# GpSimd's rotary steps at their traced pace, a fourth seven-product chunk in two stages, and q, k ahead of V in the second mixer

## The chip, the core and the metric

The kernel runs on one core of one Trainium2 chip, in one launch. The metric is the device time of that launch in microseconds. A core has TensorE (PE, with its weight loads as PEld), VectorE (DVE), ScalarE (ACT), GpSimd (POOL) and SyncE (SP), each with an in-order queue of its own, and 16 DMA engines that all queues share.

## The reference

A two-layer streaming encoder on 256 tokens of width 1024, in f32, with a memory of 256 entries. Cut to what matters:

```python
for i in range(2):
    x = x + 0.5 * swiglu(rmsnorm(x), gate, up, down)             # 1024 -> 2816 -> 1024
    q, k, v, q_m = split(rmsnorm(x) @ w_in[i], [768, 1536, 2304])
    k_m, v_m = split(rmsnorm(mem) @ w_mem_kv[i], 2)
    o_m = memory_attention(norm(q_m), norm(k_m), v_m)             # 4 heads of 64
    if i == 0:
        o_s = chunked_attention(norm(q), norm(k), v, rel_bias)    # 12 heads
    else:                                                         # 6 heads of two halves
        q, k = rotary(norm(q), positions), rotary(norm(k), positions)
        o_s = norm(softmax(q1 k1) v - lam * softmax(q2 k2) v)
    x = x + concat(o_s, o_m) @ w_out[i]
    x = x + 0.5 * swiglu(rmsnorm(x), gate2, up2, down2)
```

The rotary angles are position times inverse frequency, reduced by 2 pi, then sine and cosine.

## The kernel before

**Products.** Every large product is done in f32 by three passes: both sides are split into a high half `hi` (rounded to fp32r by ScalarE, line 417) and a low half `lo` (the rest, by VectorE, line 438), and TensorE adds hi x hi, hi x lo and lo x hi into one PSUM bank (`dense`, lines 596, 599, 602, each 128 x 128 by 512 columns). Weights come by DMA in chunks of 1 MB into 3 raw buffers; split chunks stand in 4 pairs of hi and lo buffers.

**Stages.** For each layer: FFN 1 (gate and up products, then `down` over 11 chunks), the mixer, FFN 2. A stage is named (layer, 1 or 2). In the first layer the keys and values of the memory for both layers (`memory_kv`) stand between FFN 1 and the mixer; their left sides are `memh` and `meml`. A down chunk is 8 `dense` steps, 24 matmuls. For chunks named in `SEVEN` it is done by seven products in place of eight (a Strassen-like form; `seven`, 21 matmuls, left side `h`): `seven_forms` and `seven_item` form the sums of both sides on VectorE, and `seven_sums` puts the results together. The down product ends with the last three chunks for one quarter of the result after the other, so those three stay in their weight buffers until the end.

**Mixer.** `proj` runs five projections of 512 columns for both token blocks, in the order of `WI`: q and k heads of group 0, V, q and k of groups 1 and 2, the rest of V with the memory query. Each result is normed (`head_norm`: a square on ScalarE, a sum on VectorE, a power step `hf` on GpSimd, line 639, then `qkn` on VectorE, line 1127) and turned by PE (line 632). In layer 1 q and k get their rotary step before that (`m`). Eight `unit` threads do the attention of a group and token block; three may run at a time. Products with V are line 1696 in layer 0 and line 1753 in layer 1. Then comes the output projection (left side `oT`).

**Rotary set-up.** `rope_setup` works out the reduced angles in some hundred small GpSimd steps on `ropew` (128 x 64), of which `frac` (lines 1334 and 1336) is the last pair, then two Sins on ScalarE (lines 1367 and 1368) and the tables `ropeC` and `ropeS` on VectorE. `lambda_exp` follows with an Exp. `table_hint` (line 1111) loads ScalarE's table of functions ahead of a stage: Silu for FFNs, Exp for mixers. The tables are used in layer 1 alone.

**What sets the order.** The kernel's Python is a planner: `Flow` keeps a clock `now` that goes by PE's matmuls, and the time at which each other engine is free by reckoned durations. Threads (generators) yield the time or condition at which they go on; each instruction is put into its engine's queue when the clock gets there. `flow.pool(0.25)` reckons a GpSimd step at 0.25 us, and what waits for it goes on 0.14 us (`HOP_E`) later. So a wrong reckoning changes no result, only the place of an instruction in its in-order queue. `Banks` hands out the 8 PSUM banks; a bank given back is free at once on the planner's clock.

Of the kernel before, what the change touches and what calls it, by code (L numbers as in the profile page):

```python
# [20 lines left out]
P = 128  # L21
# [29 lines left out]
class Flow:  # L51
# [3 lines left out]
    def __init__(self):  # L55
        self.now = 0.0
        self.free = {"A": 0.0, "V": 0.0, "G": 0.0}
        self.threads = []
        self.idle = []
# [49 lines left out]
    def _advance(self, limit=None):  # L109
        c = [th[0] for th in self.threads + self.idle if not callable(th[0])] + list(self.free.values())  # L110
        c = [t for t in c if t > self.now]
# [59 lines left out]
class Banks:  # L171

    def __init__(self, tile):
        self.tile, self.free, self.held = tile, list(range(8)), {}

# [4 lines left out]
    def has(self, n=1):  # L182
        return lambda: len(self.free) >= n

# [3 lines left out]
    def _hold(self, view, bs):  # L188
        for b in bs:
            self.free.remove(b)  # L190
        self.held[id(view)] = (view, bs)
        return view

    def take(self, shape):
        b = self.free[0]
        n = math.prod(shape[1:])
        view = self.tile[:, b, 0:n]
        if len(shape) == 3:
            view = view.rearrange("p (a c) -> p a c", a=shape[1])
        return self._hold(view, (b,))  # L200

    def take_pair(self):
        age = self.free.index
        b = min((b for b in self.free if b + 1 in self.free), key=lambda b: max(age(b), age(b + 1)))
        return self._hold(self.tile[:, b:b + 2, :], (b, b + 1))

    def give(self, view):
        self.free += self.held.pop(id(view))[1]


@with_exitstack
def kernel(
# [24 lines left out]
    dram = ctx.enter_context(tc.tile_pool(name="dram", bufs=4, space=bass.MemoryType.DRAM))  # L237
    banks = Banks(pp.tile([P, 8, 512], F32, name="banks"))
    g4 = Slots(flow, gp, "g", 12)
# [331 lines left out]
    for l in range(DEPTH):  # L571
        plan_ffn(l, 1, ffn1_w_gate, ffn1_w_up, ffn1_w_down)
        if l == 0:
            for ll in range(DEPTH):
                plan[ll, "kv"] = [add_chunk(cols4(w_mem_kv[ll], c, 0, 512, 0)) for c in range(2)]
        plan[l, "in"] = []
        for blk in WI:
# [151 lines left out]
    def prep_rstd(xt, tb):  # L729
        s = small([P, 1], "sst")  # L730
        nc.vector.tensor_add(s, xt.ss[tb][:, 0:1], xt.ss[tb][:, 1:2])
        flow.dve(1, 0.15)
        yield from rsqrt(xt.r[tb], s, 1, 1.0 / D)
        xt.rt[tb] = flow.now
        nc.gpsimd.tensor_scalar(out=xt.rh[tb], in0=xt.r[tb], scalar1=0.5, scalar2=None, op0=ALU.mult)
        flow.pool(0.25)

# [567 lines left out]
    def rope_setup():  # L1305
# [20 lines left out]
        nc.scalar.copy(out=hr, in_=ang)  # L1326
        yield flow.act(n)
        nc.gpsimd.tensor_copy(hi, hr.bitcast(F32))
        yield flow.pool(0.25)
        nc.gpsimd.tensor_sub(lo, ang, hi)  # L1330
        yield flow.pool(0.25)

        def frac(dst, src):
            nc.gpsimd.tensor_scalar(out=b, in0=src, scalar1=MAGIC, scalar2=MAGIC, op0=ALU.add, op1=ALU.subtract)  # L1334
            yield flow.pool(0.25)
            nc.gpsimd.tensor_sub(dst, src, b)  # L1336
            yield flow.pool(0.25)

        left = Fraction(TWO_PI_INV_NUM, TWO_PI_INV_DEN)
        first = True  # L1340
        for piece in range(5):
# [3 lines left out]
            for part in (hi, lo):  # L1345
                nc.gpsimd.tensor_scalar(out=a, in0=part, scalar1=float(cval), scalar2=None, op0=ALU.mult)
                yield flow.pool(0.25)
                nc.gpsimd.tensor_scalar(out=fa, in0=a, scalar1=2.0 ** -12, scalar2=MAGIC, op0=ALU.mult, op1=ALU.add)
                yield flow.pool(0.25)
                nc.gpsimd.tensor_scalar(out=fa, in0=fa, scalar1=MAGIC, scalar2=4096.0, op0=ALU.subtract, op1=ALU.mult)  # L1350
                yield flow.pool(0.25)
                nc.gpsimd.tensor_sub(a, a, fa)
                yield flow.pool(0.25)
                if first:
                    yield from frac(acc, a)
                    first = False
                else:
                    yield from frac(fa, a)
                    nc.gpsimd.tensor_add(acc, acc, fa)
                    yield flow.pool(0.25)  # L1360
# [3 lines left out]
        yield flow.pool(0.25)  # L1364
        yield from frac(a, a)
# [48 lines left out]
    def mixer(l, xt, gc_next):  # L1414
# [39 lines left out]
        def qk_evac(c):  # L1454
            def run(ps, tb, t):
# [5 lines left out]
                if not typ_a:  # L1461
# [6 lines left out]
                    for hf in range(2):  # L1468
# [9 lines left out]
                    nc.vector.tensor_add(m1, m1, m2)  # L1478
# [152 lines left out]
        def attn_soft(passes, done, vsrc, vready, grp, tb, bias_t, nk):  # L1631
# [35 lines left out]
            nc.vector.reciprocal(out=rs, in_=sums)  # L1667
            flow.dve(4)
            pts = [None, None]
# [39 lines left out]
        def attn_diff(passes, done, vsrc, vready, grp, tb, nk):  # L1709
# [125 lines left out]
        for c, tb in ((0, 0), (0, 1), (1, 0), (1, 1), (2, 0), (3, 0), (2, 1), (3, 1)):  # L1835
            flow.spawn(unit(c, tb))
        proj(0, qk_evac(0))
        flow.until(g4.has(2))
        take_v()
        proj(1, v_evac)  # L1840
        proj(2, qk_evac(1))
        proj(3, qk_evac(2))
        proj(4, vq_evac)

# [182 lines left out]
```

## Time and profile before

| | |
|---|---|
| median of 3 runs | 951.9 us (950.87 to 952.27) |
| the profiled execution, device time | 952.73 us |
| its span, first to last instruction | 950.8 us |
| mean granted clock of TensorE | 0.996 |
| TensorE busy | 939.5 us (99%) |
| VectorE busy | 820.6 us (86%) |
| ScalarE busy | 582.2 us (61%) |
| GpSimd busy | 110.1 us (12%) |
| DMA, mean | 220 GB/s |

A row of a timeline gives start and duration in us, engine, line and operation, the tiles written and read, the shape, and in brackets the idle time before it and what ended that. A row of a stretch gives its bounds, its length, the busy time of PE, PEld, DVE, ACT and POOL with the number of instructions, the granted clock, the busy share of the DMA engines and GB/s. Matmuls overlap: what one costs is the distance from one start to the next. A wait on an engine that nobody needs costs nothing; a wait of PE does.

### The profile page before, as it was taken

What the parts mean: (1) busy time and instruction counts of PE and PEld (TensorE: products, weight loads), DVE (VectorE), ACT (ScalarE), POOL (GpSimd) and SP (SyncE); (2) the same over time, 40 slices, a digit from 0 to 9 for tenths busy, and PEclk for the clock granted to TensorE, in tenths of its full rate; (3) what the DMA queues carried; (4) which work ended last, traced back from release to release, by engine and by line L of the source; (5) the groups of instructions that cost most, each with busy time, mean ns of one, the idle gap of its engine ahead of it and who ended that gap; (6) DMA issues with size and microseconds to landing.
All of it is one profiled execution on the core that took longest, in us unless ns stands there. A gap on an engine that the chain in (4) does not pass through costs nothing.

```text
span 950.8 us, 13163 instructions
## 1 busy us (share of the span) xinstructions
PE 939.5 (99%) x4445; PEld 771.2 (81%) x4445; DVE 820.6 (86%) x1378; ACT 582.2 (61%) x1087; POOL 110.1 (12%) x170
## 2 busy tenths in 40 slices
PE   9999999989999999999999999999999999999998
PEld 7888888767878888888888888888787788888887
DVE  6988969589998889988888999797989888998896
ACT  6655567367777656557645656564677865655661
POOL 1000048522210000000000000000325100000000
PEclk9999999989999999999999999999999999999999
DMA  9877798389746367796747779775632377589651
GB/s 298 271 251 238 233 341 290 122 280 296 242 152 217 124 220 249 238 319 209 229 132 226 235 227 296 242 243 161 218 120 90 102 242 232 184 273 305 219 185 53
DMA packets 176830, 209.27 MB, mean 220 GB/s; under 512 B 12601, under 2 KB 150650, under 8 KB 176762
## 3 DMA queue, kind: packets, MB, share of 16 engines
q1 hardware_dynamic: 168378, 202.92, 65.5%
q10 hardware_dynamic: 8384, 5.51, 1.8%
q8 instruction: 35, 0.57, 0.3%
q14 instruction: 33, 0.27, 0.1%
HBM read 191.62 MB, written 16.78 MB: 219 GB/s over the span
## 4 chain that ended last, share of the span: by engine, by line
PE 76%; DVE 10%; DMA 5%; POOL 5%; issue 2%; ACT 1%; SPq 1%; ACTq 0%; DVEq 0%
PE banks L596 22%; PE banks L602 22%; PE banks L599 22%; DVE lo L438 4%; PE banks L632 2%; PE banks L619 2%; DMA raw<-in_ffn_w_up_dram 2%; POOL ropew L1334 1%; PE banks L1604 1%; PE banks L625 1%; PE banks L1696 1%; POOL ropew L1336 1%; DMA xr<-xd 1%; ACT hi L417 1%; SPq L368 1%
## 5 line engine op out<-in xcount | busy, mean ns | idle before, releaser
L438 DVE TENSOR_TENSOR lo<-raw,hi 128x512 fp32r<-128x512 f32 (+1 forms) x466 | 388.9, 871 | 44.1 <-ACT hi L417 43.8
L417 ACT CAST hi<-raw 128x512 fp32r<-128x512 f32 (+1 forms) x465 | 333.8, 768 | 148.2 <-PE banks L602 68.2
L596 PE MATMUL banks<-hi,xh 128*128 128x512 f32 x736 | 288.8, 392 | 0.0
L599 PE MATMUL banks<-lo,xh 128*128 128x512 f32 x736 | 288.0, 391 | 0.5 <-DVE lo L1921 0.5
L602 PE MATMUL banks<-hi,xl 128*128 128x512 f32 x736 | 287.3, 390 | 0.0
L599 PEld LDWEIGHTS banks<-lo,xh 128*128 128x128 f32 x736 | 138.4, 188 | 29.1 <-DVE lo L1921 1.0
L596 PEld LDWEIGHTS banks<-hi,xh 128*128 128x128 f32 x736 | 138.3, 188 | 28.6
L602 PEld LDWEIGHTS banks<-hi,xl 128*128 128x128 f32 x736 | 138.3, 188 | 28.5
L596 PE MATMUL banks<-hi,ht 128*128 128x512 f32 x270 | 105.4, 390 | 0.0
L599 PE MATMUL banks<-lo,ht 128*128 128x512 f32 x270 | 105.3, 390 | 0.0
L602 PE MATMUL banks<-hi,ht 128*128 128x512 f32 x270 | 105.2, 390 | 0.0
L417 ACT CAST hi<-wsum 128x1024 fp32r<-128x1024 f32 (+1 forms) x51 | 44.6, 890 | 29.6 <-DVE wsum L430 29.4
L639 POOL TENSOR_TENSOR xr<-v,nhalf 128x1 f32<-128x1 f32 x12 | 8.5, 711 | 454.4 <-DVE v L637 454.3
L596 PEld LDWEIGHTS banks<-hi,ht 128*128 128x128 f32 x270 | 50.7, 188 | 10.5
L602 PEld LDWEIGHTS banks<-hi,ht 128*128 128x128 f32 x270 | 50.7, 188 | 10.4
L599 PEld LDWEIGHTS banks<-lo,ht 128*128 128x128 f32 x270 | 50.7, 188 | 10.4
L805 ACT ACTIVATE sil<-banks,xr 128x256 f32<-128x256 f32 x72 | 33.8, 470 | 35.6 <-PE banks L602 33.4
L438 DVE TENSOR_TENSOR lo<-wsum,hi 128x1024 fp32r<-128x1024 f32 (+1 forms) x51 | 50.7, 1021 | 2.9 <-ACT hi L417 2.4
L838 ACT CAST ht<-hr 128x512 fp32r<-128x512 f32 x34 | 21.0, 616 | 34.0 <-DMA hr<-hd 34.0
L639 POOL TENSOR_TENSOR hf<-v,nhalf 128x8 f32<-128x8 f32 (+1 forms) x20 | 32.0, 1598 | 72.6 <-DVE v L637 72.6
L840 DVE TENSOR_TENSOR ht<-hr,ht 128x512 fp32r<-128x512 f32 x34 | 23.4, 688 | 15.9 <-ACT ht L838 15.9
L430 DVE TENSOR_TENSOR wsum<-raw,wsum 128x512 f32<-128x512 f32 (+1 forms) x36 | 32.4, 919 | 0.3
(223 smaller groups left out, 1263.7 us busy)
## 6 DMA issues: line engine op xcount, KB each, us to landing
raw<-in_ffn_w_down_dram SPq DMA_DIRECT2D x176, 256.0 KB, 4.1
raw<-in_ffn_w_gate_dram SPq DMA_DIRECT2D x81, 512.0 KB, 4.3
raw<-in_ffn_w_up_dram SPq DMA_DIRECT2D x81, 512.0 KB, 5.0
raw<-in_w_in_dram SPq DMA_DIRECT2D x32, 512.0 KB, 4.9
hd<-hb SPq DMA_DIRECT2D x44, 256.0 KB, 5.0
hr<-hd SPq DMA_DIRECT2D x44, 256.0 KB, 4.8
raw<-in_w_out_dram SPq DMA_DIRECT2D x8, 1024.0 KB, 4.8
raw<-in_w_mem_kv_dram SPq DMA_DIRECT2D x4, 1024.0 KB, 5.9
```

Source lines behind the costliest of these rows:

```text
L417: nc.scalar.copy(out=it.part(0, q, w), in_=src())
L430: nc.vector.tensor_sub(it.t[j], x(), y())
L438: nc.vector.tensor_sub(it.part(1, q, w), src(), it.part(0, q, w).bitcast(F32))
L596: nc.tensor.matmul(out=ps, lhsT=xh, rhs=wh, start=start, stop=False)
L599: nc.tensor.matmul(out=ps, lhsT=xh, rhs=wl, start=False, stop=False)
L602: nc.tensor.matmul(out=ps, lhsT=xl, rhs=wh, start=False, stop=stop)
L619: nc.tensor.matmul(out=ps, lhsT=xt.h[tb][:, kk, :], rhs=w, start=start and k == i == 0, stop=False)
L632: nc.tensor.transpose(out=dst, in_=src, identity=ident)
L639: nc.gpsimd.tensor_tensor(out=dst, in0=v[:, :n], in1=nhalf[:, :n], op=ALU.pow)
L805: nc.scalar.activation(sil[:, tb], ps[:, tb, 0:256], AF.Silu, scale=xt.r[tb])
L838: nc.scalar.copy(out=hi, in_=src)
L840: nc.vector.tensor_sub(lo, src, hi.bitcast(F32))
```

## The change

Four things, of which the first three are reckonings or tables of the planner, and all of which move instructions:

- Small GpSimd steps are reckoned at 0.56 us in place of 0.25 (in `rope_setup`, `frac`, `prep_rstd`); the rotary step of q and k at 2.4 in place of 2.1; the reciprocals of the softmax 0.1 and 0.3 higher.
- `SEVEN` has four chunks (1, 3, 5, 7) in place of three (1, 4, 7) in the stages (0, 2) and (1, 1).
- A PSUM bank that is given back is free on the planner's clock when the engine step that was reckoned last is done.
- In layer 1 `w_in` is loaded and projected in the order q and k of groups 0, 1, 2, then V, then the rest.

```diff
     def eng(self, e, dur):
-        self.free[e] = max(self.free[e], self.now) + dur
+        self.done = self.free[e] = max(self.free[e], self.now) + dur
         return self.free[e] + HOP_E
...
+    @property
+    def free(self):
+        return [b for b, t in self.given if t <= self.flow.now]
...
     def give(self, view):
-        self.free += self.held.pop(id(view))[1]
+        self.given += [(b, self.flow.done) for b in self.held.pop(id(view))[1]]
...
-    SEVEN = {(0, 1): (), (0, 2): (1, 4, 7), (1, 1): (1, 4, 7), (1, 2): (1, 3, 5, 7)}
+    SEVEN = {(0, 1): (), (0, 2): (1, 3, 5, 7), (1, 1): (1, 3, 5, 7), (1, 2): (1, 3, 5, 7)}
...
+    WI1 = (((0, 256), (768, 256)), ((256, 256), (1024, 256)), ((512, 256), (1280, 256)), ((1536, 512),), ((2048, 256), (2304, 256)))
...
         def frac(dst, src):
             nc.gpsimd.tensor_scalar(out=b, in0=src, scalar1=MAGIC, scalar2=MAGIC, op0=ALU.add, op1=ALU.subtract)
-            yield flow.pool(0.25)
+            yield flow.pool(0.56)
             nc.gpsimd.tensor_sub(dst, src, b)
-            yield flow.pool(0.25)
+            yield flow.pool(0.56)
...
-                    flow.dve(512)
-                    yield flow.pool(2.1)
+                    flow.dve(512, 0.35)
+                    yield flow.pool(2.4)
...
-            flow.dve(4)
+            flow.dve(4, 0.1)
...
-            flow.dve(4, 0.15)
+            flow.dve(4, 0.45)
...
+        for i, k in enumerate(("q0", "v", "q1", "q2", "w") if typ_a else ('q0', 'q1', 'q2', 'v', 'w')):
+            todo[k](i)
```

PE's queue loses 6 matmuls, DVE's and ACT's gain the sums and halves of two seven-product chunks, and ACT's gains two table loads. In the order below `hi_0_...`, `lo_0_...` and `raw_...` are buffers of weights, and the lines of the kernel after are 5 higher.

ScalarE at the end of the first FFN, before: the memory's left sides and a chunk of weights, then the two Sins (1367, 1368), then the load of the Exp table.

```order
L1212 ACTIVATE memh_1713<-mr,gcol 128x256
L417 CAST hi_0_1719<-raw_1565 128x512 x2
L1212 ACTIVATE memh_1713<-mr,gcol 128x256
L1212 ACTIVATE memh_1714<-mr,gcol 128x256 x2
L1367 ACTIVATE ropew<-ropew 128x64
L1368 ACTIVATE ropew<-ropew 128x64
L1111 ACT_TABLE_LOAD
L1111 ACTIVATE dummy<-dummy 128x1
L1212 ACTIVATE memh_1714<-mr,gcol 128x256
L417 CAST hi_0_1793<-raw_1647 128x512
```

After, the Sins (1372, 1373) stand in the first mixer, between the squares `sq` of the two token blocks of its first projection (1123), with a table load of their own, and one for the Exp of `le`.

```order
L1123 ACTIVATE sq<-banks,xr 128x512
L421 CAST hi_0_2240<-raw_2131 128x512
L1283 ACTIVATE km_1896<-kr,gcol 128x256
L421 CAST hi_0_2240<-raw_2131 128x512
L1283 ACTIVATE km_1896<-kr,gcol 128x256
L421 CAST hi_0_2240<-raw_2131 128x512 x2
L1372 ACT_TABLE_LOAD
L1372 ACTIVATE ropew<-ropew 128x64
L1373 ACTIVATE ropew<-ropew 128x64
L1123 ACTIVATE sq<-banks,xr 128x512
L1412 ACT_TABLE_LOAD
L1412 ACTIVATE le<-le 128x2
```

So nothing of the memory stage stands behind the Sins any more. GpSimd at the end of the rotary steps, before: all of them, then the power steps of the first mixer's norms (`xr`) and of the memory's and the mixer's heads (`hf`).

```order
L1334 TENSOR_SCALAR ropew<-ropew 128x64
L1336 TENSOR_TENSOR ropew<-ropew 128x64
L639 TENSOR_TENSOR xr<-v,nhalf 128x1
L735 TENSOR_SCALAR xrh<-xr 128x1
L639 TENSOR_TENSOR xr<-v,nhalf 128x1
L735 TENSOR_SCALAR xrh<-xr 128x1
L1431 MEMSET bias_1939 64x4x64
L639 TENSOR_TENSOR hf<-v,nhalf 128x4
```

After, the last rotary steps stand between these power steps, and the very last one behind the `hf` of the mixer's first q and k (128x8).

```order
L644 TENSOR_TENSOR hf<-v,nhalf 128x4
L1341 TENSOR_TENSOR ropew<-ropew 128x64
L1364 TENSOR_TENSOR ropew<-ropew 128x64
L1339 TENSOR_SCALAR ropew<-ropew 128x64
L1341 TENSOR_TENSOR ropew<-ropew 128x64
L1368 TENSOR_SCALAR ropew<-ropew 128x64
L1339 TENSOR_SCALAR ropew<-ropew 128x64
L644 TENSOR_TENSOR hf<-v,nhalf 128x8
L1341 TENSOR_TENSOR ropew<-ropew 128x64
```

The work is the same, in another place of the queue. PE at the first transposes of the first mixer, before: they stand four matmuls ahead of the chunk `hi_0_2188`.

```order
L596 MATMUL banks<-hi_0_2153,xh_1783 128x512
L599 MATMUL banks<-lo_0_2154,xh_1783 128x512
L632 MATMUL banks<-ident,qkn 128x128 x4
L602 MATMUL banks<-hi_0_2153,xl_1785 128x512
L596 MATMUL banks<-hi_0_2153,xh_1783 128x512
L599 MATMUL banks<-lo_0_2154,xh_1783 128x512
L602 MATMUL banks<-hi_0_2153,xl_1785 128x512
L596 MATMUL banks<-hi_0_2188,xh_1783 128x512
```

After, they stand three matmuls behind the beginning of that chunk (now `hi_0_2184`).

```order
L607 MATMUL banks<-hi_0_2122,xl_1736 128x512
L601 MATMUL banks<-hi_0_2184,xh_1734 128x512
L604 MATMUL banks<-lo_0_2185,xh_1734 128x512
L607 MATMUL banks<-hi_0_2184,xl_1736 128x512
L637 MATMUL banks<-ident,qkn 128x128 x4
```

They moved 7 matmuls later. In the second mixer the first transposes of `m` move 4 matmuls later in the same way, and the first product with V from the end of the second projection into the fourth, which is now V's.

More of the change, by code (lines that the diff above doesn't have):

```diff
@@ L55, in __init__ @@
     def __init__(self):
-        self.now = 0.0
+        self.now = self.done = 0.0
         self.free = {"A": 0.0, "V": 0.0, "G": 0.0}
@@ L110, in _advance @@
         c = [th[0] for th in self.threads + self.idle if not callable(th[0])] + list(self.free.values())
-        c = [t for t in c if t > self.now]
+        c = [t for t in c + [self.done] if t > self.now]
         if limit is not None:
@@ L171, with __init__ @@
 class Banks:
-    def __init__(self, tile):
-        self.tile, self.free, self.held = tile, list(range(8)), {}
+    def __init__(self, flow, tile):
+        self.flow, self.tile, self.held = flow, tile, {}
+        self.given = [(b, 0.0) for b in range(8)]
+    @property
+    def free(self):
+        return [b for b, t in self.given if t <= self.flow.now]
     @property
@@ L182, in has @@
     def has(self, n=1):
-        return lambda: len(self.free) >= n
+        return lambda: self.left >= n
     def has_pair(self):
@@ L188, in _hold @@
     def _hold(self, view, bs):
-        for b in bs:
-            self.free.remove(b)
+        self.given = [g for g in self.given if g[0] not in bs]
         self.held[id(view)] = (view, bs)
@@ L194, in take @@
     def take(self, shape):
-        b = self.free[0]
+        b = (self.free or [g[0] for g in self.given])[0]
         n = math.prod(shape[1:])
@@ L237 @@
     dram = ctx.enter_context(tc.tile_pool(name="dram", bufs=4, space=bass.MemoryType.DRAM))
-    banks = Banks(pp.tile([P, 8, 512], F32, name="banks"))
+    banks = Banks(flow, pp.tile([P, 8, 512], F32, name="banks"))
     g4 = Slots(flow, gp, "g", 12)
@@ L576 @@
         plan[l, "in"] = []
-        for blk in WI:
+        for blk in WI if l == 0 else WI1:
             ids = []
@@ L735, in prep_rstd @@
         nc.gpsimd.tensor_scalar(out=xt.rh[tb], in0=xt.r[tb], scalar1=0.5, scalar2=None, op0=ALU.mult)
-        flow.pool(0.25)
+        flow.pool(0.56)
     final = []
@@ L1836, in mixer, with with_v @@
             flow.spawn(unit(c, tb))
[L1837 to L1843, printed above, removed]
+        room = [False]
+        def with_v(i, evac):
+            if not room[0]:
+                flow.until(g4.has(2))
+                take_v()
+                room[0] = True
+            proj(i, evac)
+        todo = dict(q0=lambda i: proj(i, qk_evac(0)), q1=lambda i: proj(i, qk_evac(1)), q2=lambda i: proj(i, qk_evac(2)),
+                    v=lambda i: with_v(i, v_evac), w=lambda i: with_v(i, vq_evac))
+        for i, k in enumerate(("q0", "v", "q1", "q2", "w") if typ_a else ('q0', 'q1', 'q2', 'v', 'w')):
+            todo[k](i)
         flow.until(banks.has(4))
```

24 lines of the change are left out of this document (12 added, 12 removed).

## The prediction

> **What bounds the kernel.** I read the page first, then the waits, the stretches and the order of time of the stage where the waits are.
>
> ```profile
> span 950.8 us, 13163 instructions
> PE 939.5 (99%) x4445; PEld 771.2 (81%) x4445; DVE 820.6 (86%) x1378; ACT 582.2 (61%) x1087; POOL 110.1 (12%) x170
> ```
>
> TensorE is busy 99% of the span. Its matmuls overlap, so a busy share does not say how fast they start. The start-to-start time does. These are the first row of the seven-product chunk 1 of the first layer's second down stage, and the first row after its 21 matmuls:
>
> ```profile
> 438.92 0.39 PE L596 MATMUL banks<-hi,h 128*128 128x512 f32 x1
> ...
> 443.68 0.39 PE L596 MATMUL banks<-hi,ht 128*128 128x512 f32 x1
> ```
>
> 4.76 us for 21 starts is 0.2267 us each. That is the price of one 512-column matmul wherever PE isn't held up, and a stage is lost time only where starts are further apart. So two things can move the end: fewer matmuls, and fewer stalls. The longest stall lies around 190 us. The waits of the stretch from 165 to 215 us (engine, line, whom it waited for; us in total, times, longest):
>
> ```profile
> ACT ropew L1367 <- POOL ropew L1336: 10.1, 1, 10.1
> DVE ropeC L1377 <- ACT ropew L1368: 8.1, 1, 8.1
> PE banks L596 <- ACT hi L417: 2.8, 1, 2.8
> ACT hi L417 <- DMA xd<-xb: 2.8, 1, 2.8
> ACT xh L705 <- DVE y L697: 2.7, 2, 2.4
> ```
>
> ScalarE stands 10.1 us at the first Sin of the rotary set-up, because GpSimd has not finished the angles, and VectorE stands 8.1 us at the first rotary table behind it. The stretches show that nothing else was done meanwhile (columns: length, busy time of PE, PEld, DVE, ACT, POOL, granted clock, DMA share, GB/s):
>
> ```profile
> 175.00:180.00 5.00, 5.00 (x24) 4.14 (x23) 0.00 (x0) 0.26 (x1) 4.08 (x12) 1.00 0.10 37
> 190.00:195.00 5.00, 2.24 (x4) 1.45 (x5) 4.97 (x15) 2.90 (x7) 0.83 (x2) 0.61 0.92 315
> ```
>
> PE lives on its split weights until about 187 us, then runs dry at 190 to 195, and the granted clock falls to 0.61. TensorE in order of time, the memory keys and values: the first row, the stall, the first and the last row at the low clock, and the first row of the projection behind them, with the group that counts one of the three kinds of matmul there.
>
> ```profile
> 185.65 0.39 PE L596 MATMUL banks<-hi,memh 128*128 128x512 f32 x1
> ...
> 188.79 0.40 PE L602 MATMUL banks<-hi,meml 128*128 128x512 f32 x1
> 191.99 0.79 PE L596 MATMUL banks<-hi,memh 128*128 128x512 f32 x1 [2.81 <-ACT hi L417]
> 193.56 0.79 PE L599 MATMUL banks<-lo,memh 128*128 128x512 f32 x1 [0.77 <-DVE lo L438]
> 194.15 0.63 PE L602 MATMUL banks<-hi,meml 128*128 128x512 f32 x1
> ...
> 197.98 0.39 PE L602 MATMUL banks<-hi,meml 128*128 128x512 f32 x1
> ...
> 216.37 0.39 PE L596 MATMUL banks<-hi,xh 128*128 128x512 f32 x1
> ...
> L596 PE MATMUL banks<-hi,memh 128*128 128x512 f32 x32 | 13.6, 425 | 2.8 <-ACT hi L417 2.8
> ```
>
> **The change, part by part.**
>
> Rotary pace. GpSimd's steps run from the first to the last of these rows, 51.8 us for some hundred of them, or 0.50 us each:
>
> ```profile
> 128.91 0.52 POOL L1328 COPY ropew<-ropehr 128x64 f32<-128x64 f32 x1 [14.24 <-ACT ropehr L1326]
> ...
> 180.36 0.32 POOL L1336 TENSOR_TENSOR ropew<-ropew 128x64 f32<-128x64 f32 x1
> ```
>
> The planner reckoned 0.25 plus its hop of 0.14, so it put the Sins some 12 us too early into ScalarE's queue. With 0.56 plus 0.14 it errs to the late side: both Sins and the tables now stand behind the first query and key evacuation of the first mixer. There GpSimd's last step is queued directly behind that evacuation's power step, so the second Sin waits for little. What it frees: the memory stage takes 216.37 - 185.65 = 30.72 us for 3 x 32 = 96 matmuls; at 0.2267 they take 21.76. The loss is 8.96 us. It ends if the splits of the four memory weight chunks come in time. The first two of them stood behind the Sins and behind the residual sums that VectorE did late. With both engines free from 169 us the limit is the weight slots instead, which the last 18 down matmuls before 185.65 free one by one, and the round trip of x through DRAM that shares ScalarE's queue (rival 1). PE needs the second chunk 12 matmuls, 2.7 us, after 185.65, and the third 8 us after that, so I take the whole 8.96; ends 4.8 (with rival 1) and 8.96. DMA does not take it back: the 0.92 above is its catching up after the 0.10, and one 1 MB chunk per 24 matmuls is 1 MB per 5.4 us, 193 GB/s. In SP's queue a few loads change places with a neighbour, and w_in's blocks their order, at the DMA shares of 0.6 to 0.84 that the rows below show; I cost that at nothing.
>
> Table loads. The Sins used to run before the table change to Exp. Behind it, they need a load of their own, and the Exp that follows needs another. The load that exists:
>
> ```profile
> 181.00 1.28 ACT L1111 ACT_TABLE_LOAD   x1
> 182.29 0.20 ACT L1111 ACTIVATE dummy<-dummy 128x1 f32<-128x1 f32 x1
> ```
>
> Start to next start it is 1.29 us, so two loads are 2.6 us of ScalarE around the second block's evacuation, which the planner does not reckon. What waits behind: the squares of the second token block, and through them its transposes on PE. ScalarE ahead of those squares, and PE's transposes at their end:
>
> ```profile
> 226.15 1.66 ACT L417 CAST hi<-raw 128x512 fp32r<-128x512 f32 x3 [1.30 <-DMA raw<-in_w_in_dram]
> ...
> 230.25 0.62 ACT L417 CAST hi<-raw 128x512 fp32r<-128x512 f32 x1 [1.11 <-DMA raw<-in_w_in_dram]
> 230.78 0.69 ACT L1118 ACTIVATE sq<-banks,xr 128x512 f32<-128x512 f32 x1
> ...
> 236.97 0.64 PE L632 MATMUL banks<-ident,qkn 128*128 128x128 f32 x4
> ```
>
> PE did not wait there. The squares stood behind 1.30 + 1.11 = 2.4 us of waits for weights, late from the stall. Without it the weights come in time, and 2.6 in place of 2.4 us leaves it even: I take 0, ends 0 (work is only added) and +2.6. On VectorE the first rotary tables and nlam wait for a Sin or for the second load, under 1.3 us each, with halves of weights behind them that PE uses a chunk, 5.4 us, later. The Trainium skill (ScalarE: Activation LUTs, What ACT_TABLE_LOAD costs) gives about 1.28 us for the load, and about 1.38 us more to drain, 2.66 us for each switch; the row agrees with the first figure and shows nothing of the second, since the next instruction starts 1.29 us after the load. By the page's figure the estimate for two would be 5.3 us, and the sum below up to 2.7 us higher.
>
> First transposes of the first mixer. They waited:
>
> ```profile
> 228.83 0.39 PE L599 MATMUL banks<-lo,xh 128*128 128x512 f32 x1
> 229.85 0.66 PE L632 MATMUL banks<-ident,qkn 128*128 128x128 f32 x4 [0.63 <-DVE qkn L1127]
> ```
>
> 1.02 us instead of the 0.31 of an undisturbed switch (below). They now stand 7 matmuls, 1.6 us, later: -0.71 us. Ends -0.71 and 0.
>
> Seven products. Two stages get a fourth such chunk: 21 matmuls for 24, twice, is 6 x 0.2267 = -1.36 us. The price is VectorE's: four differences of weights and three more halves, each of 512 elements, and small sums of the left side. A group of that size, then stretches of the first layer's second down stage, which has three such chunks, and of the last layer's, which has four already:
>
> ```profile
> L840 DVE TENSOR_TENSOR ht<-hr,ht 128x512 fp32r<-128x512 f32 x34 | 23.4, 688 | 15.9 <-ACT ht L838 15.9
> ...
> 440.00:450.00 10.00, 10.00 (x45) 8.28 (x45) 9.96 (x17) 7.55 (x15) 0.00 (x0) 1.00 0.84 272
> 470.00:480.00 10.00, 10.00 (x46) 8.29 (x45) 6.97 (x10) 4.67 (x7) 0.00 (x0) 1.00 0.73 229
> 920.00:930.00 10.00, 10.00 (x46) 8.29 (x45) 10.00 (x18) 7.49 (x14) 0.00 (x0) 1.00 0.61 202
> ```
>
> Seven at 0.69 are 4.8 us a chunk. In the last stretch VectorE is full and PE still gets all its 10 us, with four chunks at the same places; and the stage that is changed has room at 470. So I cost the extra work at nothing; its cover is the 4 split chunks that PE has ahead. Ends -1.36 and, if the 4.8 us a stage came out on PE, +8.2.
>
> Second mixer and banks. PE's waits there, from 660 to 775 us:
>
> ```profile
> PE banks L632 <- DVE m L1478: 0.7, 2, 0.4
> PE banks L632 <- DVE oT L1569: 0.2, 1, 0.2
> ```
>
> 0.9 us is all that an order can win. The first transposes now come 4 matmuls later, which covers the larger half of the wait for m; the rest is a draw. I take -0.5; ends -0.9 and +2 (each of five new breaks, counted below, with a wait as long as the 0.4). V's chunks go behind q and k; the first product with V comes some 100 PE rows later. Banks that count as free only when their reader is reckoned done move PE's rows by a few places in both mixers, and break its runs of projection matmuls 4 and 1 times more often. A break, against a long run of transposes:
>
> ```profile
> 291.77 1.91 PE L632 MATMUL banks<-ident,pe 128*128 128x128 f32 x16
> 293.61 1.09 PE L1696 MATMUL banks<-tr,V 128*64 128x128 f32 x16
> ...
> 302.92 0.60 PE L632 MATMUL banks<-ident,pe 128*128 128x128 f32 x4
> 303.27 0.48 PE L596 MATMUL banks<-hi,oT 128*128 128x512 f32 x1
> 303.59 0.60 PE L632 MATMUL banks<-ident,pe 128*128 128x128 f32 x4
> ```
>
> Four transposes take 0.35 us to the next start, and the matmul behind them 0.32 instead of 0.2267; with the same on the way in, a break costs 0.18. Five are 0.9 us. The sixteen in a row took 1.84 instead of 4 x 0.35 = 1.40, and they are split up now: -0.4. Together +0.5 us. The remaining reckonings (reciprocals, m) only move rows, which is in these figures.
>
> **The sum.** -8.96 - 1.36 - 0.71 - 0.5 + 0.5 = -11.0 us. The profiled execution took 952.73 us (its span, and 1.9 around it), so 941.7; it lies 0.8 over the median of the runs, 951.9. I predict 941.0.
>
> **Rivals.**
>
> 1. The stall returns behind the x round trip. ScalarE's queue holds the reading back of x, which waits for its writing; the two waits for these transfers above are 2.8 and 2.4 us (the longest), with splits queued behind. Against it: they were taken in a stretch with DMA at 0.92, and the splits have 2.7 to 13 us of room. If PE stood 2.4 us, and the clock fell as it did after 2.8 (from 194.15 to 197.98 nine gaps at 0.43 instead of 0.23, +1.8), it would cost 4.2: 945.2. The Trainium skill (TensorE: Matmul & The Clock Gate, What's actually happening) lets the clock fall after an idle window of about 3.4 us; the trace shows it falling after 2.81. By the page the rival would cost 2.4, 943.4.
> 2. VectorE can't carry the fourth chunks. The 9.96 and 10.00 speak for it, PE's full 10 us beside them against it. Price up to 4.8 us in each stage: 941.0 + 9.6 = 950.6.
> 3. Slower: V last leaves attention without cover. The first V chunks come two projections, 2 x 48 matmuls or 21.8 us, later. If those 21.8 us came out behind the last projection matmul, where PE has only the output projection, the time would be 962.8; it is slower than before once 11 us of them do. Against it: behind the last projection matmul PE's order holds 4 products with V, as before.
> 4. The weights are still late at the second block's squares, and the two loads come on top of those waits: 2.6 us on PE's transposes there, 943.6. For it speaks that PE's transposes had nothing to spare, against it that DMA no longer catches up. By the page's drain the same place would cost an estimated 2.7 us even with the weights in time.
>
> **Chances and range.** The forecast 0.78, rival 1 0.11, rival 2 0.03, rival 3 0.04, rival 4 0.04. The forecast's own spread comes from the ends: all small terms good, 941.0 - 0.4 (waits of the second mixer) - 0.5 (breaks) - 0.7 (runs differ by 1.4 us) = 939.4; the mixer at +2 in place of -0.5, 943.5. Rival 1 with such a draw gives up to 946. Range 939.2 to 945.5. Under 0.2% (1.9 us) is no difference that a measurement of this kernel can tell. Faster: the forecast, rivals 1 and 4, and two thirds of rival 2, 0.95; slower three quarters of rival 3, 0.03; the rest is the same, 0.02.
>
> **What would show it.** No wait of ScalarE or VectorE over 2 us between 169 and 185 us; the memory stage in 21.8 to 22.5 us with clock 1.00; two more table loads, 1.3 us each, about 10 us before the first scores, and no wait of PE for qkn over 0.3 us there; 60 us down stages shorter by 0.7 us with no PE wait; the second mixer within 2 us of its 103 us. I am wrong if PE still pauses among the memory matmuls, or if new waits of over 2 us stand in either mixer.

## The result, and the profile after

| | before | after |
|---|---|---|
| median of 5 runs each, on one chip | 952.12 us (950.87 to 954.47) | 944.27 us (942.76 to 944.75) |
| the profiled execution | 952.73 us | 942.83 us |
| mean granted clock | 0.996 | 1.000 |

The ratio is 0.9909, with a 95% interval of 0.9893 to 0.9925: the change makes the kernel faster by 0.9%. The prediction was 941.0 us with 939.2 to 945.5; the median lies 3.3 us above the one and within the other. The runs after fall in two groups, two near 942.8 and three near 944.5, and the profiled execution is one of the lower group. One run of a kernel further down, of before with the sevens alone, took 2429.5 us and is in neither its median nor its ratio.

The busy times, as for before: six matmuls fewer, and 12.5 us more work on VectorE.

```profile
span 941.0 us, 13206 instructions
PE 935.3 (99%) x4439; PEld 768.4 (82%) x4439; DVE 833.1 (89%) x1404; ACT 588.2 (63%) x1099; POOL 114.7 (12%) x170
```

TensorE in order of time, the first and the last row of the memory stage and the row behind it:

```profile
185.66 0.39 PE L601 MATMUL banks<-hi,memh 128*128 128x512 f32 x1
...
207.20 0.39 PE L607 MATMUL banks<-hi,meml 128*128 128x512 f32 x1
207.42 0.39 PE L601 MATMUL banks<-hi,xh 128*128 128x512 f32 x1
```

207.42 - 185.66 = 21.76 us for 96 matmuls, 0.2267 each: there is no stall left (before: 30.72). The two stretches in which before had VectorE at nothing or a low clock, then the whole down stage (0, 2) with its fourth chunk of seven products, and 10 us of it:

```profile
175.00:180.00 5.00, 5.00 (x24) 4.13 (x22) 3.44 (x6) 1.29 (x4) 0.10 (x1) 1.00 0.63 184
190.00:195.00 5.00, 5.00 (x24) 4.14 (x23) 4.93 (x12) 3.92 (x9) 3.15 (x6) 1.00 1.01 344
424.60:483.13 58.53, 58.53 (x265) 48.43 (x264) 55.71 (x97) 35.78 (x67) 0.78 (x2) 1.00 0.61 200
461.10:471.10 10.00, 10.00 (x46) 8.28 (x45) 9.86 (x17) 4.77 (x7) 0.00 (x0) 1.00 0.75 239
```

The same stage before:

```profile
433.48:492.72 59.24, 59.24 (x269) 49.03 (x267) 50.23 (x83) 33.09 (x61) 0.79 (x2) 1.00 0.60 198
```

PE is busy throughout in all of them, though VectorE now has 55.71 us of work in the stage where it had 50.23. The stage begins 8.9 us earlier than before, so the place that stood at 470 now stands at 461.10: there VectorE has 9.86 us where it had 6.97. All of PE's waits in the whole span (engine, line, whom for; us in total, times, longest):

```profile
PE banks L1901 <- DVE junk L1896: 1.0, 1, 1.0
PE banks L604 <- DVE lo L442: 0.5, 1, 0.5
PE banks L604 <- DVE lo L1932: 0.4, 1, 0.4
PE banks L637 <- DVE pe L1747: 0.2, 1, 0.2
```

The first and third are in the first 9 us, where before has them too (1.0 and 0.5). Only the 0.5 and the 0.2 are in a mixer, both in the second.

### The profile page after: what moved, and what is told of

It is laid out like the page before. It is cut to its first block, busy times and chain, and to the rows that moved or that the text cites. A ratio compares the mean times of both kernels' runs of the same rounds, so it can differ in the third digit from the quotient of the medians.

```text
span 941.0 us, 13206 instructions
## 1 busy us (share of the span) xinstructions
PE 935.3 (99%) x4439; PEld 768.4 (82%) x4439; DVE 833.1 (89%) x1404; ACT 588.2 (63%) x1099; POOL 114.7 (12%) x170
## 4 chain that ended last, share of the span: by engine, by line
PE 97%; DVE 3%; issue 0%; ACT 0%; DVEq 0%
PE banks L601 29%; PE banks L607 29%; PE banks L604 29%; PE banks L637 2%; PE banks L624 2%; PE banks L1609 1%; PE banks L630 1%; PE banks L1701 1%; DVE lo L442 1%; PE banks L1758 0%; PE banks L1901 0%; DVE qkn L1132 0%; DVE m L1483 0%; DVE m L1479 0%; DVE hss L1126 0%
## 5 line engine op out<-in xcount | busy, mean ns | idle before, releaser
L601 PE MATMUL banks<-hi,ht 128*128 128x512 f32 x254 | 99.1, 390 | 0.0
L607 PE MATMUL banks<-hi,ht 128*128 128x512 f32 x254 | 99.0, 390 | 0.0
L604 PE MATMUL banks<-lo,ht 128*128 128x512 f32 x254 | 98.9, 390 | 0.0
L607 PEld LDWEIGHTS banks<-hi,ht 128*128 128x128 f32 x254 | 47.7, 188 | 9.9
L601 PEld LDWEIGHTS banks<-hi,ht 128*128 128x128 f32 x254 | 47.7, 188 | 9.7
L604 PEld LDWEIGHTS banks<-lo,ht 128*128 128x128 f32 x254 | 47.7, 188 | 9.7
L434 DVE TENSOR_TENSOR wsum<-raw,wsum 128x512 f32<-128x512 f32 (+1 forms) x40 | 35.2, 895 | 0.4
L845 DVE TENSOR_TENSOR ht<-hr,ht 128x512 fp32r<-128x512 f32 x32 | 21.8, 683 | 9.8 <-ACT ht L843 9.8
```

The costliest lines, as they stand in the source:

```text
L434: nc.vector.tensor_sub(it.t[j], x(), y())
L601: nc.tensor.matmul(out=ps, lhsT=xh, rhs=wh, start=start, stop=False)
L604: nc.tensor.matmul(out=ps, lhsT=xh, rhs=wl, start=False, stop=False)
L607: nc.tensor.matmul(out=ps, lhsT=xl, rhs=wh, start=False, stop=stop)
L845: nc.vector.tensor_sub(lo, src, hi.bitcast(F32))
```

## Where the time came from

For all kernels below one table is used. Its columns are stages, each from its first PE start to the next stage's first PE start: the memory stage, the two mixers, and the down stages (0, 2) and (1, 1). What the table doesn't hold is 600.3 to 601.2 us in each.

| kernel | memory | mixer 1 | down (0, 2) | down (1, 1) | mixer 2 | profiled |
|---|---|---|---|---|---|---|
| before | 30.72 | 99.66 | 59.24 | 59.25 | 103.18 | 952.73 |
| after | 21.76 | 99.74 | 58.54 | 58.54 | 103.64 | 942.83 |
| before + pace | 21.76 | 101.38 | 59.25 | 59.23 | 103.22 | 945.60 |
| before + pace + bank rule | 21.80 | 99.63 | 59.25 | 59.25 | 104.84 | 946.00 |
| before + bank rule | 32.86 | 100.98 | 59.23 | 59.24 | 104.85 | 957.81 |
| before + sevens | 28.67 | 99.79 | 58.53 | 58.67 | 106.55 | 952.88 |
| before + Sins held | 22.57 | 99.40 | 59.23 | 59.24 | 103.70 | 944.76 |
| after - pace | 29.92 | 100.70 | 58.55 | 58.56 | 103.64 | 952.07 |
| after - order q, k, V | 21.86 | 100.12 | 58.53 | 58.52 | 103.64 | 943.11 |
| after - bank rule | 23.32 | 101.21 | 58.55 | 58.54 | 104.43 | 946.38 |
| after + Sins held | 22.59 | 99.50 | 58.55 | 58.53 | 103.57 | 943.67 |

From before to after: memory -8.96, the two down stages -1.41, the mixers +0.08 and +0.46, together -9.83; the profiled executions differ by 9.90.

## The experiments

Ratios are to the kernel before, run beside it on the same chip.

**The pace alone.** Before, with `pool(0.25)` reckoned at 0.56 everywhere in the rotary set-up and in `prep_rstd`:

```diff
-            yield flow.pool(0.25)
+            yield flow.pool(0.56)
```

> The kernel before with the small GpSimd steps reckoned at 0.56 us, and nothing else of the change. Theory A (the gain is the Sins' place in ScalarE's queue): the memory stage falls from 30.72 to 21.8 us, the three-chunk down stages stay at 59.2, the mixers stay within 1 us of 99.7 and 103.2; the time falls by 8.5 to 9.3 us, to 0.990 to 0.991 of before. Theory B (the stall ends only together with the new bank rule or the other reckonings): the memory stage keeps 3 us or more of its 9 us loss and the gain is under 6 us.

945.53 us, ratio 0.9927 (0.9915 to 0.9940). The memory stage is at 21.76, as after, so the pace alone takes away the whole stall. Of its 8.96 us 1.72 are given back in the first mixer. Theory A is right about the stall, but it had the mixers within 1 us of before, and so 8.5 to 9.3 us of gain where 7.1 came.

**After without the pace.** The same lines back at 0.25 in the kernel after:

> The kernel after with the small GpSimd steps reckoned at 0.25 us again. Theory A (the Sins' place alone makes the memory stage's stall): ScalarE waits some 10 us at the Sins again, the memory stage takes 28 to 31 us, and 7 to 9 us of the gain are lost: ratio to before 0.998 to 1.002. Theory B (the bank rule or the other reckonings help ScalarE out of it): the memory stage stays under 25 us.

952.0 us, ratio 0.9997 (0.9987 to 1.0007): without the pace nothing is left of the gain that can be measured. Its waits from 165 to 215 us are those of before, with other lengths:

```profile
ACT ropew L1372 <- POOL ropew L1341: 8.7, 1, 8.7
...
DVE ropeC L1382 <- ACT ropew L1373: 6.1, 1, 6.1
...
PE banks L601 <- ACT hi L421: 2.2, 1, 2.2
```

**The Sins held back by hand.** If the stall comes from the place of the Sins and not from the pace as such, then before with nothing but the Sins moved must lose it too. Here the Sins and the tables wait until the first layer's second FFN begins, the Exp for `lambda` until the second mixer, and the pace stays at 0.25. Cut to the line that holds the Sins:

```diff
+            yield lambda: stage[0] >= 2
             nc.scalar.activation(...)   # the two Sins
```

> The kernel before, pace 0.25 and all else as it was, but the thread of the rotary set-up holds its two Sins and the tables back until the first layer's second FFN, and the Exp for lambda until the second mixer; so neither Sin needs a table load of its own. Theory A (only the Sins' place counts, not the reckoned pace of the steps ahead of them): memory stage 21.8 us, gain as with the pace alone, 6.5 to 9 us. Theory B (the reckoned pace also has to set the places of the power steps on GpSimd): memory stage above 24 us.

945.74 us, ratio 0.9935 (0.9918 to 0.9952); memory stage 22.57. The gain, 6.0 us, is a little under the 6.5 expected, and 0.8 us stay in the memory stage (see the bank rule below for what they are). So the place is the cause: GpSimd's steps are reckoned as wrongly as before and run where they ran. ScalarE at the first Sin, with no load of its own for either, since both stand behind the load that the FFN has anyway:

```profile
308.97 1.28 ACT L1112 ACT_TABLE_LOAD   x1
310.37 0.24 ACT L1369 ACTIVATE ropew<-ropew 128x64 f32<-128x64 f32 x1
```

**The same hold in the kernel after.** It takes the two table loads out of the first mixer, and so prices them:

> The kernel after with the Sins, the tables and the Exp for lambda held back in the same way: the two table loads of 1.28 us in the first mixer are gone, and so are the tables' 16 small steps on VectorE there. Theory A (the loads lie beside other work): the first mixer stays within 0.4 us of 99.74. Theory B (they delay the second token block): it falls by 1 to 2.6 us.

943.41 us (942.09 to 943.67), ratio 0.9906 (0.9891 to 0.9920), against 0.9909 for after; the first mixer takes 99.50 for 99.74. The two loads cost nothing that can be measured.

**The sevens alone.** Before with the new `SEVEN` line and nothing else:

> The kernel before with the fourth seven-product chunk in the two down stages, and nothing else. Theory A: the two down stages fall from 59.2 to 58.5 us each, the memory stage stays at 30.7, and the time falls by 1.4 us (ratio 0.9985). Theory B (VectorE can't carry them once the rest of the plan is the old one): new waits of PE for lo in the down stages or at the start of the FFN or mixer behind them, and no gain.

954.75 us, ratio 1.0025 (1.0014 to 1.0036). The two down stages are 0.71 and 0.58 us shorter, as theory A has it, and yet the kernel is slower; the waits for lo that theory B names did not come either. The second mixer is 3.37 us longer. PE's waits there, 650 to 780 us:

```profile
PE banks L1753 <- DVE o L1769: 1.1, 1, 1.1
PE banks L632 <- ACT PT L1618: 0.9, 2, 0.5
PE banks L632 <- DVE m L1478: 0.9, 2, 0.5
```

2.9 us of waits where before has 0.9, and four breaks more in PE's runs of dense matmuls (40 for 36). Nothing in that mixer was edited: six matmuls fewer move the planner's clock, with it the rows.

**The order of q, k and V.** After, with the projections of the second mixer in the old order:

```diff
-        for blk in WI if l == 0 else WI1:
+        for blk in WI:
...
-        for i, k in enumerate(("q0", "v", "q1", "q2", "w") if typ_a else ('q0', 'q1', 'q2', 'v', 'w')):
+        for i, k in enumerate(("q0", "v", "q1", "q2", "w")):
```

> The kernel after with the old order of the second mixer's projections (q and k of group 0, V, then the rest). Theory A (q and k ahead of V gives nothing, it costs the 0.5 us that the second mixer became longer): the second mixer takes 103.0 to 103.4 us in place of 103.64, the rest as after; ratio to before 0.9885 to 0.991. Theory B (the order wins, and the new bank rule or the reckonings lose): the second mixer becomes longer than 104 us.

943.65 us, ratio 0.9906 (0.9891 to 0.9922). The second mixer takes 103.64 us with V last and 103.64 with V second: this part of the change does nothing that can be seen, and neither theory had the number. Up to 676 us every engine of this kernel has its instructions in the order of after, and yet its first mixer takes 100.12 us for 99.74: 0.4 us is what one execution differs from another there.

**The bank rule, three times.** After without it; before with it and the pace; before with it alone:

```diff
-        self.given += [(b, self.flow.done) for b in self.held.pop(id(view))[1]]
+        self.free += self.held.pop(id(view))[1]
```

> The kernel after with PSUM banks free at once on the planner's clock when they are given back, as before. Theory A (the bank rule moves rows and wins nothing that can be seen): each mixer within 0.4 us of after (99.7 and 103.6). Theory B (the bank rule is what keeps PE from waiting for evacuations): new waits of PE on banks in the mixers, together over 1 us.

946.28 us, ratio 0.9936 (0.9919 to 0.9953): 2.0 us lost between the medians; in the profiled executions 1.5 in the first mixer, 0.8 in the second and 1.6 in the memory stage. PE's new waits, for a `pe` of ScalarE, are 0.5 and 0.6 us, so theory B is met, if barely. By this alone the rule would be a gain of its own.

The 1.6 us of the memory stage are not the rule's. Up to 242 us every engine has its instructions in the order of before + pace, which has the old rule too and takes 21.76 us there. What differs is the execution: ScalarE stands 6.55 us at the turned x (before + pace: 5.03), the halves behind it come later, and PE waits twice for one, 0.59 and 0.15 us:

```profile
186.64 0.62 ACT L417 CAST hi<-raw 128x512 fp32r<-128x512 f32 x1 [6.55 <-DMA xd<-xb]
201.59 0.50 PE L600 MATMUL banks<-lo,memh 128*128 128x512 f32 x1 [0.59 <-DVE lo L438]
```

This is the prediction's rival 1 in small: no fall of the clock, but 1.6 us. Before + Sins held shows it too (ScalarE 6.66 us at x, and PE's only wait there, 0.43): its 0.8 us are that.

> The kernel before with the pace of 0.56 and the new bank rule, without the fourth chunks, the new order and the other reckonings. With the pace alone the first mixer took 101.4 us, and without the bank rule the kernel after took 101.2 there, against 99.7 with all. Theory A (the bank rule wins back what the moved rows lose in the first mixer): first mixer 99.6 to 100.2, memory stage 21.8, time 1 to 2 us under that with the pace alone. Theory B (those 1.5 us come from chance places of rows that any change moves): first mixer above 100.7.

945.81 us, ratio 0.9937 (0.9924 to 0.9950), the same as with the pace alone. The rule takes back the 1.7 us in the first mixer, as theory A has it, and puts 1.6 on the second, so theory A's 1 to 2 us of time did not come.

> The kernel before with the new bank rule alone; the Sins stay in the memory stage. Theory A (the bank rule by itself gains about 2 us in the mixers, as the kernel after without it suggested): first mixer below 98.5 us, 950 us or less. Theory B (any order of rows lands the mixers somewhere in a spread of some 2 us, and the rule has no gain of its own): first mixer 99.4 to 100.1, second 103.2 to 104.9, memory stage 29 to 31, and 951.5 to 954.

954.74 us, ratio 1.0026 (1.0014 to 1.0037). Theory A, a gain of its own, falls: both mixers are longer, by 1.32 and 1.67 us. Theory B had the size of the second mixer, but set the first 0.9 us and the memory stage 1.9 us too low, and so the median by 0.7. PE's largest single wait in the second mixer is the same in this kernel and the one before it, 1.6 us for a `pe` of ScalarE.

**More sevens.** The down stage (0, 1) has none. If VectorE can carry them there as it does in the others, 1.4 to 2.0 us are to be had. After with:

```diff
-    SEVEN = {(0, 1): (), ...
+    SEVEN = {(0, 1): (4, 7), ...      # and (3, 5, 7), and (5, 7)
```

> The kernel after with two seven-product chunks (4, 7) in the first layer's first down stage too, which has none. If VectorE and the weights carry them there: the stage from 59.84 to 58.48, 6 matmuls fewer, and 942.9. Rival: VectorE, which also does the memory's norms between 155 and 175 us (10.0 of 10 us busy), hands halves over late: PE waits for lo in the stage or in the memory stage of over 0.5 us, and the time is 944 to 947. Second rival: the shift of the planner's clock by 1.4 us puts the mixers elsewhere in their spread, 942 to 945.

> As the run before it, with three such chunks (3, 5, 7): the stage 57.8, 942.2 if carried. Rival: chunk 7 falls beside VectorE's full stretch, a wait of PE for lo or for ht over 0.5 us, 944 to 948.

> As the two before it, with the chunks (5, 7), both in VectorE's full stretch: 942.9 if carried; if VectorE is the limit, this one is slower than (4, 7) by the more, 944 to 948.

956.91, 959.44 and 955.93 us, ratios 1.0041 (1.0024 to 1.0059), 1.0078 (1.0061 to 1.0094) and 1.0044 (1.0027 to 1.0061): all slower than before, by far more than the rivals' 944 to 948, and with (5, 7) no worse than (4, 7), so the third expectation missed its order too. The kind of wait is the one named, VectorE's halves. With (4, 7) PE pauses at the second matmul of the memory stage:

```profile
189.46 0.39 PE L601 MATMUL banks<-hi,memh 128*128 128x512 f32 x1
194.09 0.70 PE L604 MATMUL banks<-lo,memh 128*128 128x512 f32 x1 [4.24 <-DVE lo L442]
```

VectorE in that time, without a gap: PE's next `lo` (193.35) stands behind residual sums, left sides of the memory and turns of x.

```profile
189.28 0.75 DVE L756 SCALAR_TENSOR_TENSOR x<-banks,xrh,x 128x512 f32<-128x512 f32 x1
189.94 0.61 DVE L1221 SCALAR_TENSOR_TENSOR meml<-mr,gcol,memh 128x128 fp32r<-128x128 f32 x2
190.47 2.08 DVE L683 STREAM_TRANSPOSE xb<-x 128x512 f32<-128x512 f32 x2
192.45 0.73 DVE L756 SCALAR_TENSOR_TENSOR x<-banks,xrh,x 128x512 f32<-128x512 f32 x1
...
193.35 0.68 DVE L442 TENSOR_TENSOR lo<-raw,hi 128x512 fp32r<-128x512 f32 x1
```

With (3, 5, 7) the stretches show VectorE full and PE, in the last of them, at almost nothing:

```profile
155.00:165.00 10.00, 7.86 (x35) 6.19 (x33) 9.96 (x27) 7.84 (x18) 9.01 (x16) 1.00 0.75 245
165.00:175.00 10.00, 9.03 (x32) 6.99 (x33) 10.00 (x17) 8.06 (x16) 8.77 (x16) 0.83 0.40 117
175.00:185.00 10.00, 0.56 (x3) 0.14 (x1) 9.86 (x23) 5.87 (x13) 8.44 (x20) 0.77 0.54 198
```

The down stage takes 75.78 us for the 59.84 of after, and the memory stage behind it a clean 21.75; with (4, 7) they take 63.67 and 33.60, with (5, 7) 61.64 and 33.92. VectorE's debt comes out in the one stage or in the other. No kernel here beats after by more than the intervals tell; with the Sins held it is as fast.

## Why the prediction was right, and where its sum was off

- **Memory stage, -8.96.** Measured -8.96, with clock 1.00. The mechanism is shown from three sides: the pace alone ends the stall, its removal brings it back, and the Sins held back by hand end all but 0.8 us of it without the pace. That the size fits to the hundredth is because the loss was read from the one execution that it is compared with; others with the Sins in their old place took 28.67 to 32.86 us (last section). One reading was off: PE ran dry at 189.2 us, behind its row at 188.79, not at about 187.
- **Seven products, -1.36.** Measured -0.70 and -0.71. VectorE carried them without a wait of PE, as the stretches of that stage say. Rival 2 is wrong for these stages and right for the first down stage, where VectorE is already at 10.00 of 10 from 155 to 175 us in after and has little room for 4.8 us a chunk; the three kernels with sevens there show what comes of it.
- **Table loads, 0.** Right. Both stand where the order had them:

```profile
218.83 1.28 ACT L1372 ACT_TABLE_LOAD   x1
220.12 0.26 ACT L1372 ACTIVATE ropew<-ropew 128x64 f32<-128x64 f32 x1
220.29 0.24 ACT L1373 ACTIVATE ropew<-ropew 128x64 f32<-128x64 f32 x1
220.43 0.67 ACT L1123 ACTIVATE sq<-banks,xr 128x512 f32<-128x512 f32 x1
221.12 1.28 ACT L1412 ACT_TABLE_LOAD   x1
222.42 0.20 ACT L1412 ACTIVATE le<-le 128x2 f32<-128x2 f32 x1
```

  The Trainium skill (ScalarE: Activation LUTs, What ACT_TABLE_LOAD costs) adds about 1.38 us of draining to each load of about 1.28 us. These rows agree with the 1.28; the next instruction starts 1.29 and 1.30 us after a load starts, so no draining is seen, and rival 4's extra 2.7 us by that page did not come.
- **First transposes, -0.71.** The wait is gone. The step to them fell from 1.02 to 0.23 us, a little more than forecast, and they take 0.35 us themselves:

```profile
221.48 0.39 PE L607 MATMUL banks<-hi,xl 128*128 128x512 f32 x1
221.71 0.60 PE L637 MATMUL banks<-ident,qkn 128*128 128x128 f32 x4
222.06 0.48 PE L601 MATMUL banks<-hi,xh 128*128 128x512 f32 x1
```

- **Mixers, -0.5 and +0.5: this is the step that failed.** With the -0.71 they were to bring -0.7 and brought +0.54. The number of breaks was right: 27 for 23 in the first mixer and 37 for 36 in the second, and five at 0.18 are the 0.9 of the sum. The 0.18 was a little high: the matmul ahead of transposes keeps its 0.23 us, as the rows above show, and only the one behind them takes 0.32; the matmul that the prediction read for the way in (303.27) stood behind transposes as well. In the first mixer the matmuls on both sides of the four more breaks took 0.6 us more, 0.15 a break. What did not come are the two gains set against them: the -0.4 for splitting up sixteen transposes (the small products of the first mixer take about 19.3 us after and 19.2 before), and the -0.5 in the second mixer, where 0.85 us of waits became 0.64, on other rows. Without these two the sum is -8.96 - 1.36 - 0.71 + 0.9 = -10.1, against 9.9 measured. That is near, but in the second mixer not by its parts: one break more and 0.2 us less of waits make about nothing, and 0.46 came. Where that half microsecond lies stays open.
- **The offset of the profiled execution.** The prediction took 0.8 us off because before's profiled execution lay that far above its median. After's lies 1.4 below its own. So of the 3.3 us by which the median is off, 1.1 are the stages' (942.83 against 941.7) and 2.2 are this offset of one execution to its median, which the range had to hold and did.
- **The signs to look for.** Met: the memory stage in 21.8 us at clock 1.00, two loads of 1.28 us about 10 us before the first scores (230.92), no wait for `qkn`, the down stages 0.7 shorter, the second mixer within 2 us of 103. Not met as written: no wait of ScalarE or VectorE over 2 us before 185. From 165 to 208 us there are these:

```profile
ACT junk L727 <- DVE x L756: 5.1, 2, 3.0
ACT hi L421 <- DVE xb L683: 4.9, 1, 4.9
DVE x L756 <- POOL ropew L1339: 2.0, 1, 2.0
```

  They cost nothing in this execution, since PE starts every 0.2267 us through the whole stage; a wait of another engine was too strict a sign for a claim on PE.
- **Rivals 1 and 3.** The round trip of x did not stop PE in the traced execution of after. It did for 1.6 us in that of after without the bank rule, which has the same order of instructions up to there, so rival 1 was not refuted; only its clock term and its size did not show. The slower group of after's runs lies 1.7 us above the faster; whether that is the same stop isn't shown, since none of that group was traced. V behind q and k left no attention uncovered, and gained nothing either.

**What the parts are worth.** Each part's effect on a mixer depends on which others are there. The first mixer comes before any stage in which the sevens differ, and pace and bank rule sort its times, beside the 0.4 us between executions of one order:

| first mixer | old bank rule | new bank rule |
|---|---|---|
| pace 0.25 | 99.66, 99.79, 99.40 (Sins held) | 100.70, 100.98 |
| pace 0.56 | 101.38, 101.21 | 99.63, 99.74, 100.12, 99.50 (Sins held) |

In the second the sevens and the bank rule sort them: with the old rule 103.18, 103.22 and 103.70 (Sins held) without the sevens, 106.55 and 104.43 with them; with the new rule 104.84 and 104.85 without, 103.57 (Sins held) and 103.64 three times with them. So in either mixer one of its two parts alone lengthens it by 1 to 3 us and both together by none to half a microsecond. But under the new rule the sevens came only together with the remaining reckonings (the rotary step of q and k, the reciprocals), and no run has these alone; the 1.2 us between 104.84 and 103.64 can be theirs as well. The numbers repeat between kernels built apart, by more than the 0.4 us that one order differs from itself, so this is the order of rows, which each part deals anew. Why a given order is better than another is open: the runs show waits and breaks, not a rule. "The bank rule is worth 2 us", which the first of its three experiments seemed to say, is not a statement that holds.

## What to carry to other kernels

In an order that a planner sets by reckoned times, look first for a step that is reckoned too short and sits in the in-order queue of an engine that feeds others: two Sins put into ScalarE's queue some 10 us too early cost 9 us of TensorE, and moving them to either of two later places gave nearly all of it back. Price such a part by undoing it in the kernel after and doing it alone in the kernel before; where the two disagree, as with the bank rule, the part has no price of its own. Compare the orders of the queues before a difference between two traces is put down to an edit: 1.6 us of the memory stage came and went between two kernels with one order. Cutting matmuls pays only as far as the engine that prepares the replacement has room in that very stage: 0.7 us a stage here, and 12 to 15 us lost where VectorE was already full.

## What the runs showed of the hardware

**The clock after a pause of PE.** Before's pause of 2.81 us was followed by nine gaps at 0.43 us. The other kernels give a series. After the 2.68 us and another 0.96 us (before with the sevens), half pace:

```profile
191.29 0.60 PE L596 MATMUL banks<-hi,memh 128*128 128x512 f32 x1 [2.68 <-ACT hi L417]
192.85 0.79 PE L599 MATMUL banks<-lo,memh 128*128 128x512 f32 x1 [0.96 <-DVE lo L438]
193.44 0.63 PE L602 MATMUL banks<-hi,meml 128*128 128x512 f32 x1
193.87 0.63 PE L596 MATMUL banks<-hi,memh 128*128 128x512 f32 x1
```

After 2.16 us and another 1.06 (after without the pace), full pace:

```profile
190.75 0.49 PE L601 MATMUL banks<-hi,memh 128*128 128x512 f32 x1 [2.16 <-ACT hi L421]
192.30 0.50 PE L604 MATMUL banks<-lo,memh 128*128 128x512 f32 x1 [1.06 <-DVE lo L442]
192.63 0.39 PE L607 MATMUL banks<-hi,meml 128*128 128x512 f32 x1
192.87 0.39 PE L601 MATMUL banks<-hi,memh 128*128 128x512 f32 x1
```

And after 10.17 us (with the chunks 3, 5, 7), half pace, but for no longer than after 2.68:

```profile
185.73 0.80 PE L604 MATMUL banks<-lo,ht 128*128 128x512 f32 x1 [10.17 <-DVE lo L442]
186.32 0.63 PE L607 MATMUL banks<-hi,ht 128*128 128x512 f32 x1
...
190.59 0.43 PE L601 MATMUL banks<-hi,ht 128*128 128x512 f32 x1
190.86 0.39 PE L604 MATMUL banks<-lo,ht 128*128 128x512 f32 x1
```

Half pace lasts from about 186 to 190.6 here, 10 gaps of 0.43 us or some 2 us lost; after 2.68 us there are 11 such gaps. In all nine pauses of 2.68 us or more the loss was 4 to 11 gaps, 0.8 to 2.2 us on top of the pause; after pauses of 2.16 us or less there was none. The sum of neighbouring pauses does not decide it: 2.16 and 1.06 left full pace, 2.92 and 0.19 (same kernel as the last) brought half pace, and not at once: the first two steps behind the 2.92 us still took 0.34 and 0.24.

```profile
165.78 0.50 PE L604 MATMUL banks<-lo,h 128*128 128x512 f32 x1 [2.92 <-DVE lo L442]
166.95 0.79 PE L604 MATMUL banks<-lo,h 128*128 128x512 f32 x1 [0.19 <-DVE lo L442]
```

The Trainium skill (TensorE: Matmul & The Clock Gate, What's actually happening) names a window of about 3.4 us that runs freely, so that its place against the pause would matter; no trace here shows the window. The clock fell in these runs after pauses shorter than it.

**The stall's own spread.** With the Sins in their old place ScalarE's wait for them was 8.6, 8.7, 10.1 and (before with the bank rule) 12.5 us, and the memory stage took 28.67, 29.92, 30.72 and 32.86 us, in the same order. The size of the gain there is thus a matter of the single execution: from 7 to 11 us. The runs of the kernel before, too, go from 949.6 to 954.7.
